# Loading and multiplying the late modulation weights in steps between the projections of a two-layer diffusion transformer

## The chip, the cores and the metric

The kernel runs as one program on one core of one Trainium2 chip. The time of a kernel is the device time of one execution in microseconds; three runs of the kernel before lie within 2729.07 to 2732.03 us, with a median of 2731.18 us. TensorE is called PE below, VectorE DVE, ScalarE ACT, GpSimd POOL, and SyncE, which issues the transfers spoken of here, SP.

## What is computed

Two layers (`DEPTH = 2`) work on 1024 tokens and 256 context tokens of 1024 features in fp32. Cut to what matters:

```python
for l in range(DEPTH):
    m_lat = jnp.split(_adaln(c, w_mod[l], b_mod[l])[:, None, :], N_MOD, axis=-1)
    m_ctx = jnp.split(_adaln(c_ctx, w_mod[l], b_mod[l]), N_MOD, axis=-1)
    h = _modulate(_rmsnorm(x, norm1_w[l]), m_lat[0], m_lat[1])
    hc = _modulate(_rmsnorm(cx, norm1_w[l]), m_ctx[0], m_ctx[1])
    mix, mix_c = _token_mixers(h, hc, w_in[l], ...)
    x = x + m_lat[2] * jnp.einsum('btm,md->btd', mix, w_out[l])
    h2 = _modulate(_rmsnorm(x, norm2_w[l]), m_lat[3], m_lat[4])
    x = x + m_lat[5] * _expert_choice_ffn(h2, w_router[l], ...)
    ...
def _adaln(cond, w, b):
    return jnp.matmul(jax.nn.silu(cond), w) + b
def _modulate(h, shift, scale):
    return h * (1 + scale) + shift
```

`w_mod[l]` is 1024 x 6144. Its six column blocks of 1024 give, for two condition vectors, the shift and scale of the first norm (part 0 in the kernel), the gate of the mixers and the shift of the second norm (part 1), and the scale of the second norm and the gate of the experts (part 2). Only part 0 is needed before the mixers; parts 1 and 2 are first used after the attention, when `w_out` has been applied. The mixers are a projection by `w_in`, a gated linear recurrence (three pairs of heads), a short convolution, and an attention over a neighbourhood of 8 x 16 (three pairs of heads).

## The kernel before

The main loop (lines 1430 to 1500) takes a layer in stages. First the normed and modulated tokens are kept transposed as a high and a low half (`hh`, `hl`), so that a product in fp32 is made of three products in a faster format. **Projections:** `wgroup` (L243) loads a group of 256 columns of `w_in` in two halves of 512 KB (tile `wst`, three buffers), ACT casts each half to `whi` (L264), DVE subtracts to `wlo` (L265). `proj_ch` (L277) or `proj_tok` (L288) then run 24 matmuls per output tile, `pj`, and ACT or DVE moves the result out through tiles of the ring `ev` (three buffers, `nev` at L566) to DRAM. There are 15 such groups: two for the recurrence's values (the first one's weights are loaded ahead), six for its three pairs, three for the convolution, and four, in `na_proj` (L585), for the attention. The recurrence (`hg_pair`: `hl`, `hds`, `ho`, then the mean of squares `hms` at L504 in the PSUM bank "E", its root and reciprocal `hrs`, and the output `hos`) runs beside the projections of what follows.

**Attention:** `na_consts` (L591) loads the norm weights `naw` and the rotation tables `cw` and `sw`; `na_prep` (L647) loads queries and keys `qk`, norms and rotates them on DVE and POOL (`nss`, `nrs...`, `qn`, `qd`) and has PE transpose them (`nt`, L697). `na_pair` (L771) makes scores (`sA`, `sB`), adds the bias on DVE (L743), takes the exponential on ACT (L750), transposes (`npt`) and multiplies by the values (`nao`). The preparation of the next pair is written behind each pair and overlaps with it. After pair 0 and the preparation of pair 1 stands `adaln(l, [1, 2], ap)`: two parts of eight steps (k = 0 to 7), each with two loads of 512 KB of `w_mod` (tile `wm`, L153, four buffers in a pool of its own that is opened after the projections' pools are closed) and four matmuls `aps` of 128 x 512 (L157; eight records in the trace) in the four column groups of PE, then the sum with the bias (`ms`, L166, with `bt`, L160 to 162), its store, and transposes and copies to `mt` and `AB` (L168 to 178). The part 0 of layer 0 is made at the program's start, that of layer 1 among the experts of layer 0.

The order on each engine is set by a scheduler at build time: it may move an instruction ahead of others on its engine, but every engine then runs its own list strictly in that order, and waits on semaphores for the others. A tile of a ring can be filled only when the use of the tile before it in the same buffer is over. In order of time the stages of the profiled execution are: projections and recurrence of layer 0 from 22 to 616 us, pair 0 to 722, pair 1 to 794; in layer 1 from 1500 to 2010, 2142 and 2218 us.

## Time and profile before

| | before |
|---|---|
| median of three runs | 2731.18 us |
| the profiled execution's own time | 2732.13 us |
| span of its profile | 2730.4 us |
| PE busy | 2504.4 us (92%) |
| DVE busy | 1884.3 us (69%) |
| ACT busy | 1131.4 us (41%) |
| POOL busy | 669.3 us (25%) |
| moved by DMA | 507.12 MB, 186 GB/s in the mean |

Busy time is the time in which an engine ran at least one instruction, as a share of the span; matmuls overlap, and the end of one is modelled, so that a busy PE need not be at its peak. An engine's share is a mean over stages that have different limits: what a change is worth is read from the rows of the stretches that it touches.

### The profile page before, as it was taken

The page shows a single profiled execution, that of the slowest core. Times are in us where ns is not written, and L with a number is a line of the kernel's source. Part 1 is how long each engine was busy: PE and PEld are TensorE (multiplying, and loading weights), DVE is VectorE, ACT ScalarE, POOL GpSimd, SP SyncE. Part 2 cuts the span into 40 slices and gives each one's busy share as a digit, 9 for nine tenths or more (in the row PEclk, how much of TensorE's full clock was granted, in tenths as well). Part 3 has the DMA queues.
Part 4 walks back from the last instruction along what each step waited for, and adds up shares of the span by engine and source line. Part 5 has one row for each costly group of instructions (what it writes and reads, how often), then busy time and mean ns, then how long its engine had stood idle before and what let it go on. Part 6 is the DMA issues. An engine that isn't in the chain of part 4 may idle for free.

```text
span 2730.4 us, 55190 instructions
## 1 busy us (share of the span) xinstructions
PE 2504.4 (92%) x21959; PEld 1906.9 (70%) x21959; DVE 1884.3 (69%) x4046; ACT 1131.4 (41%) x1878; POOL 669.3 (25%) x621
## 2 busy tenths in 40 slices
PE   7999999998999979999996999999958899589997
PEld 4998887894677855555554988778844677367664
DVE  4258887857666586777754368787858874787874
ACT  4224433324554534444434334333314554345452
POOL 1000000035444633333311000000045532222241
PEclk9999999998999979999998999999979999789999
DMA  7332324247354948888887332423176355889994
GB/s 281 102 108 71 114 68 123 66 138 243 113 160 135 349 151 278 281 280 279 283 280 212 94 105 74 124 84 89 49 200 225 94 163 183 300 281 370 377 376 127
DMA packets 347936, 507.12 MB, mean 186 GB/s; under 512 B 53380, under 2 KB 203072, under 8 KB 346592
## 3 DMA queue, kind: packets, MB, share of 16 engines
q1 hardware_dynamic: 336416, 465.85, 50.4%
q0 software_dynamic: 11264, 37.75, 5.9%
q8 instruction: 173, 2.83, 0.4%
q14 instruction: 83, 0.68, 0.1%
HBM read 410.10 MB, written 94.90 MB: 185 GB/s over the span
## 4 chain that ended last, share of the span: by engine, by line
PE 67%; DVE 18%; DMA 5%; issue 4%; ACT 3%; POOL 2%; SPq 1%; POOLq 0%; DVEq 0%; ACTq 0%
PE pg L1280 13%; PE pj L277 12%; PE pd L1335 8%; PE pj L288 8%; PE po L828 6%; PE nao L786 3%; PE pgc L1265 2%; PE npt L762 2%; PE sA L733 1%; DVE Kt L375 1%; PE aps L157 1%; DVE Kt L376 1%; DVE Qt L378 1%; PE hl L365 1%; PE xt L1231 1%
## 5 line engine op out<-in xcount | busy, mean ns | idle before, releaser
L1182 DVE TENSOR_TENSOR ewl<-est,ewh 128x2048 fp32r<-128x2048 f32 x126 | 298.1, 2371 | 109.7 <-ACT ewh L1178 108.6
L1178 ACT CAST ewh<-est 128x2048 fp32r<-128x2048 f32 x128 | 243.4, 1905 | 170.9 <-PE pg L1280 130.5
L277 PE MATMUL pj<-hl,whi 128*128 128x320 f32 (+2 forms) x912 | 310.2, 340 | 0.0
L277 PE MATMUL pj<-hh,whi 128*128 128x320 f32 (+2 forms) x912 | 309.9, 340 | 0.0
L277 PE MATMUL pj<-hh,wlo 128*128 128x320 f32 (+2 forms) x912 | 308.7, 339 | 0.0
L288 PE MATMUL pj<-whi,hh 128*128 128x256 f32 x960 | 277.8, 290 | 4.5 <-ACT nev L566 4.1
L288 PE MATMUL pj<-whi,hl 128*128 128x256 f32 x960 | 276.8, 291 | 0.8 <-DVE hl L239 0.8
L288 PE MATMUL pj<-wlo,hh 128*128 128x256 f32 x960 | 275.5, 288 | 0.0
L1335 PE MATMUL pd<-est,hidT 128*128 128x512 f32 x512 | 232.2, 596 | 2.1 <-ACT hidT L1302 2.1
L288 PEld LDWEIGHTS pj<-whi,hh 128*128 128x128 f32 x960 | 186.0, 194 | 8.8 <-ACT nev L566 5.2
L288 PEld LDWEIGHTS pj<-wlo,hh 128*128 128x128 f32 x960 | 185.9, 194 | 2.2 <-issue 1.3
L288 PEld LDWEIGHTS pj<-whi,hl 128*128 128x128 f32 x960 | 184.6, 194 | 3.5 <-issue 1.3
L277 PEld LDWEIGHTS pj<-hh,whi 128*128 128x128 f32 x912 | 172.2, 189 | 13.7 <-issue 0.9
L277 PEld LDWEIGHTS pj<-hl,whi 128*128 128x128 f32 x912 | 172.2, 189 | 13.5 <-issue 1.9
L277 PEld LDWEIGHTS pj<-hh,wlo 128*128 128x128 f32 x912 | 172.1, 189 | 13.0 <-issue 1.1
L1335 PEld LDWEIGHTS pd<-est,hidT 128*128 128x128 f32 x512 | 95.2, 189 | 110.7 <-issue 103.3
L265 DVE TENSOR_TENSOR wlo<-wst,whi 128x1024 fp32r<-128x1024 f32 (+1 forms) x72 | 75.2, 1058 | 131.7 <-ACT whi L264 130.6
L1280 PE MATMUL pg<-ewh,xh 128*128 128x512 f32 x512 | 156.8, 424 | 3.1 <-ACT xh L1235 3.0
L752 POOL TENSOR_SCALAR S<-S,sm 128x768 f32<-128x768 f32 (+2 forms) x108 | 108.6, 1007 | 188.3 <-DVE sm L751 166.8
L1280 PE MATMUL pg<-ewl,xh 128*128 128x512 f32 x512 | 147.7, 404 | 0.0
L1280 PE MATMUL pg<-ewh,xo 128*128 128x512 f32 x512 | 142.3, 398 | 2.1 <-DVE xo L1236 2.1
L750 ACT ACTIVATE S<-S,mn 128x768 f32<-128x768 f32 (+2 forms) x108 | 98.6, 913 | 85.2 <-DVE mn L745 79.6
(369 smaller groups left out, 5560.9 us busy)
## 6 DMA issues: line engine op xcount, KB each, us to landing
est<-in_w_exp_gate_dram SPq DMA_DIRECT2D x64, 1024.0 KB
est<-in_w_exp_up_dram SPq DMA_DIRECT2D x64, 1024.0 KB
est<-in_w_exp_down_dram SPq DMA_DIRECT2D x64, 1024.0 KB
wm<-in_w_mod_dram SPq DMA_DIRECT2D x80, 512.0 KB
wst<-in_w_in_dram SPq DMA_DIRECT2D x88, 256.0 KB
pna<-nev SPq DMA_DIRECT2D x180, 64.0 KB
wos<-in_w_out_dram SPq DMA_DIRECT2D x42, 256.0 KB
mst<-mix SPq DMA_DIRECT2D x32, 320.0 KB
```

Of the source, the lines that this page charges most:

```text
L265: nc.vector.tensor_tensor(b, c, a, ALU.subtract)
L277: nc.tensor.matmul(ps[:, :cn], sel(a(k)), b[:, k, c0:c0 + cn], start=n == 0, stop=n == 3 * KD - 1)
L288: nc.tensor.matmul(ps[:, :2 * P], b[:, k, t * P:(t + 1) * P], a(k).rearrange("p a n -> p (a n)"), start=n == 0, stop=n == 3 * KD - 1)
L750: nc.scalar.activation(S[:, :w], S[:, :w], AF.Exp, scale=-1.0, bias=mn[:, 1:2], accum_out=sm[:, 0:1])
L752: nc.gpsimd.tensor_scalar(S[:, :w], S[:, :w], sm[:, 1:2], 1.0, ALU.mult, ALU.mult)
L762: nc.tensor.transpose(pt[:kn, i], S[:, c:c + kn], self.idf)
L786: nc.tensor.matmul(po[64 * X:64 * X + 64, gi], V[:kn, tt, 64 * X:64 * X + 64], PT[X][:kn, i], start=i == 0, stop=i == len(ch) - 1, tile_po ...
L828: nc.tensor.matmul(ps, a, b, start=n == 0, stop=n == len(ops) - 1)
L1178: nc.scalar.copy(hi, src)
L1182: nc.vector.tensor_tensor(lo[:, :m], src[:, :m], hi[:, :m], ALU.subtract)
L1280: nc.tensor.matmul(acc[gu], a[:, 4 * hf + k], b[:, 512 * k:512 * k + 512], start=n == 0, stop=n == 3 * KD - 1)
L1335: self.downed = nc.tensor.matmul(po[nn], hT[:, 2 * hf + k], st[:, c:c + 512], start=hf == 0 and k == 0, stop=hf == 1 and k == 1)
```

## The change

Parts 1 and 2 of the modulation are taken out of the attention. A generator, `adaln_steps`, makes one of its sixteen steps (two loads, four matmuls) each time that it is called. `wgroup` calls it once after the loads of its group, and the convolution twice more. The two tiles of a step now come from the ring `wst` of the projections' weights, `aps` accumulates in bank "E", and the bias and sum tiles `bt` and `ms` come from the ring `ev`. The mean of squares `hms` moves from bank "E" to bank "D", where `ho` is. The pool `ad1` with its four buffers is gone. The bytes loaded, the matmuls and the vector work are the same. Part 0 is computed as before.

```diff
+    def adaln_steps(self, l, wp):
+        nc, I = self.nc, self.I
+        for r in (1, 2):
+            ps = self.bank("E", [P, 512], F32, "aps")
             for k in range(KD):
                 w = []
...
+                for h in (0, 1024):
+                    t = wp.tile([P, 1024], F32, name="wm", tag="wst", bufs=3)
+                    nc.sync.dma_start(t, I["w_mod"][l, k * P:(k + 1) * P, r * 2048 + h:r * 2048 + h + 1024])
+                    w += [t[:, a:a + 512] for a in (0, 512)]
+                self.adaln_mm(ps, k, w)
+                if k == KD - 1:
+                    bt, ms = [wp.tile([P, 512], F32, name=n, tag="ev", bufs=3) for n in ("bt", "ms")]
+                    self.adaln_end(l, r, ps, bt, ms, "E")
+                yield
...
@@ def wgroup
+        next(self.side, None)
         return (lambda k: his[k // 4][:, k % 4]), (lambda k: los[k // 4][:, k % 4])
...
@@ def hg_pair
-            pm = self.bank("E", [P, 512], F32, "hms")
+            pm = self.bank("D", [P, 512], F32, "hms")
...
@@ def conv_proj
             w = self.wgroup(l, wp, c, c + P)
+            if c != CB0:
+                next(self.side)
...
@@ def mixers_in
         self.hg_consts(self.hp)
+        self.side = self.adaln_steps(l, wp)
...
@@ main loop
-        adp = K.pool(f"ad1_{l}", side="right")
-        ap = adp.__enter__()
...
-                    if p == 0:
-                        K.adaln(l, [1, 2], ap)
-            adp.__exit__(None, None, None)
```

The line numbers of the changed file differ: `aps` is L145, its loads L198, `pj` L304 and L315, `hms` L532, `nt` L727, the transfers of `naw`, `cw`, `sw`, `qk` L626 to L691.

On PE, among the recurrence's projections of layer 0, the changed kernel has at one place (a row counts an instruction, of which the trace shows two records for fp32 `aps`):

```order
L304 MATMUL pj<-hh,whi 128x320
L304 MATMUL pj<-hl,whi 128x320
L304 MATMUL pj<-hh,wlo 128x320
L145 MATMUL aps<-wm,sT 32x512 x4
L304 MATMUL pj<-hh,whi 128x320
L304 MATMUL pj<-hl,whi 128x320
```

A whole step stands there in one piece between two groups of columns; before, nothing stood between such `pj`. Of the 32 steps of both layers, most stand like this; the first two of each layer are split in halves, and a few others 1 + 3.

On PE at the end of layer 1's projections, before, behind the last `hms` come 46 `pj`, and behind the last of them:

```order
L288 MATMUL pj<-whi,hl 128x256
L157 MATMUL aps<-wm,sT 32x512 x8
L697 MATMUL nt<-idf,qd 128x128 x4
L157 MATMUL aps<-wm,sT 32x512 x8
L697 MATMUL nt<-idf,qd 128x128 x8
L157 MATMUL aps<-wm,sT 32x512 x2
```

In the changed kernel 105 `pj` come behind the last `hms`, and then:

```order
L315 MATMUL pj<-whi,hl 128x256
L727 MATMUL nt<-idf,qd 128x128 x20
L765 MATMUL sB<-KH,QT 128x256
L765 MATMUL sB<-KL,QT 128x256
L727 MATMUL nt<-idf,qd 128x128 x16
```

The modulation is gone from the first transposes of the attention, and the end of the recurrence has moved ahead, against the projections.

On SP in the same place, before, behind the last store of a projection:

```order
L510 DMA mix_15766<-hos 128x512
L869 DMA wr<-in_w_router_dram 128x8x16
L637 DMA E<-rpbx 64x14x64 x4
L596 DMA naw<-in_na_q_norm_dram 128x64
L597 DMA naw<-in_na_k_norm_dram 128x64
L609 DMA cw<-in_rope_dram 128x4x64
```

and in the changed kernel:

```order
L537 DMA mix_15762<-hos 128x512
L597 DMA pna_15763<-nev 128x128 x2
L626 DMA naw<-in_na_q_norm_dram 128x64
L627 DMA naw<-in_na_k_norm_dram 128x64
L639 DMA cw<-in_rope_dram 128x4x64
L640 DMA sw<-in_rope_dram 128x4x64
L597 DMA pna_15763<-nev 128x128 x2
```

The loads for the attention (`naw`, `cw`, `sw`) now stand ahead of the last stores of the projections, and the bias loads `E` no longer stand ahead of them.

## Rows read from the trace of the kernel before

**Rows 1.** Chain of waits, 600 to 735 us, shares of 135 us by line.

```profile
by line: PE aps L157 17.4%; PE nao L786 12.5%; PE npt L762 8.9%; POOL qd L688 6.9%; PE nt L697 6.5%; PE sA L733 6.0%; issue 4.6%; DMA qk<-pna 3.7%; PE sB L735 3.5%; DVE qn L672 3.4%; DVE QT L702 3.1%; DVE nss L664 2.6%; DVE S L743 2.5%; DMA
```

**Rows 2.** Windows: stretch, length, busy PE, PEld, DVE, ACT, POOL, clock, DMA share, GB/s.

```profile
22.00:616.00 594.00, 564.33 (x7167) 516.06 (x7166) 403.85 (x924) 229.71 (x470) 45.91 (x63) 0.99 0.37 111
1500.00:2010.00 510.00, 491.99 (x6497) 438.95 (x6495) 364.55 (x844) 186.47 (x391) 24.45 (x37) 1.00 0.30 91
...
649.00:714.00 65.00, 63.93 (x446) 35.22 (x443) 47.56 (x122) 27.90 (x54) 29.96 (x30) 1.00 0.65 211
2072.00:2111.00 39.00, 38.32 (x255) 19.99 (x255) 33.70 (x76) 16.55 (x30) 21.60 (x19) 1.00 0.65 209
```

**Rows 3.** The same windows for L157 alone: stretch, length, busy PE, PEld.

```profile
616.00:722.00 106.00, 32.09 (x128) 4.39 (x128) 0.90 0.69 214
2010.00:2142.00 132.00, 33.19 (x128) 4.59 (x128) 0.86 0.68 199
...
649.00:714.00 65.00, 24.69 (x104) 3.43 (x100) 1.00 0.65 211
2072.00:2111.00 39.00, 15.80 (x64) 2.17 (x64) 1.00 0.65 209
```

**Rows 4.** PE's waits, 100 to 616 and 1500 to 2010 us: in total, times, longest.

```profile
PE hl L341 <- DVE Qt L378: 7.5, 11, 1.3
...
PE hl L341 <- DVE Qt L378: 12.6, 17, 1.7
```

**Rows 5.** Timeline of PE: start, us, line, operation, records; half and whole steps.

```profile
659.68 1.05 PE L157 MATMUL aps<-wm,sT 128*32 128x512 f32 x4
660.66 1.09 PE L786 MATMUL nao<-PT,nav 128*64 128x128 f32 x16
...
1453.33 1.06 PE L157 MATMUL aps<-est,sT 128*32 128x512 f32 x8
...
2058.91 1.07 PE L157 MATMUL aps<-wm,sT 128*32 128x512 f32 x8
```

**Rows 6.** Timeline of ACT: exponentials of scores in pairs 0 and 1, both layers.

```profile
649.00 0.94 ACT L750 ACTIVATE S<-S,mn 128x768 f32<-128x768 f32 x1
...
706.07 0.99 ACT L750 ACTIVATE S<-S,mn 128x832 f32<-128x832 f32 x1
...
730.64 0.98 ACT L750 ACTIVATE S<-S,mn 128x768 f32<-128x768 f32 x1
...
767.81 0.99 ACT L750 ACTIVATE S<-S,mn 128x832 f32<-128x832 f32 x1
...
2072.30 0.94 ACT L750 ACTIVATE S<-S,mn 128x768 f32<-128x768 f32 x1 [4.28 <-DVE mn L745]
...
2111.59 0.99 ACT L750 ACTIVATE S<-S,mn 128x832 f32<-128x832 f32 x1
...
2149.44 0.94 ACT L750 ACTIVATE S<-S,mn 128x768 f32<-128x768 f32 x1
...
2172.60 0.99 ACT L750 ACTIVATE S<-S,mn 128x832 f32<-128x832 f32 x1 [0.88 <-DVE mn L745]
```

**Rows 7.** Timeline of PE, SP and DVE at the end of layer 1's projections.

```profile
2002.73 1.02 PE L505 MATMUL hms<-hsq,hones 128*128 128x512 f32 x2
...
2008.98 0.28 PE L288 MATMUL pj<-whi,hl 128*128 128x256 f32 x1
...
2045.23 1.11 PE L697 MATMUL nt<-idf,qd 128*128 128x128 f32 x4 [2.84 <-DVE qd L688]
...
2021.73 0.89 SPq L596 DMA_DIRECT2D naw<-in_na_q_norm_dram  x1
...
2032.08 1.06 DVE L672 TENSOR_TENSOR qn<-qk,cw 128x512 f32<-128x512 f32 x1 [4.98 <-DMA qk<-pna]
```

**Rows 8.** Timeline: one half group of weights from issue to cast.

```profile
1465.42 0.96 SPq L252 DMA_DIRECT2D wst<-in_w_in_dram  x2
...
1469.72 1.04 ACT L264 CAST whi<-wst 128x1024 fp32r<-128x1024 f32 x1 [11.28 <-DMA wst<-in_w_in_dram]
```

More of the change, by code (lines that the diff above doesn't have):

```diff
@@ L134, in bounds, with adaln_open, adaln_mm @@
         nc.vector.tensor_scalar(self.lb1, self.lb, -1.0, 1.0, ALU.mult, ALU.add)
-    def adaln(self, l, parts, ap, tag="M", bufs=4, late=None, big=None):
+    def adaln_open(self, l):
+        self.mds[l] = self.dram(f"mod{l}", [2, 6 * D])
+        self.mts[l] = self.cp.tile([P, 2, 48], F32, name=f"mt{l}")
+        self.ABs[l] = self.cp.tile([P, 2, 2, KD], F32, name=f"ab{l}")
+    def adaln_mm(self, ps, k, w):
+        for j in range(4):
+            self.nc.tensor.matmul(ps[32 * j:32 * j + 32], self.sT[:, k, :], w[j], start=k == 0, stop=k == KD - 1,
+                                  tile_position=(0, 32 * j))
@@ L139, in adaln, with adaln_end @@
+    def adaln_end(self, l, r, ps, bt, ms, tag, late=None):
         nc, I = self.nc, self.I
[L140 to L143 removed]
         md, mt, AB = self.mds[l], self.mts[l], self.ABs[l]
[L145 to L147 removed]
+        nc.gpsimd.memset(bt, 0.0)
+        for j in range(4):
+            nc.sync.dma_start(bt[32 * j:32 * j + 2],
+                              I["b_mod"][l:l + 1, (4 * r + j) * 512:(4 * r + j + 1) * 512].to_broadcast([2, 512]))
+        if late:
+            late()
+        nc.vector.tensor_tensor(ms, ps, bt, ALU.add)
+        for j in range(4):
+            nc.sync.dma_start(md[:, (r * 4 + j) * 512:(r * 4 + j + 1) * 512], ms[32 * j:32 * j + 2])
+        tp = self.bank(tag, [P, 4, P], F32, "atp")
+        for c in range(4):
+            nc.tensor.transpose(tp[:, c], ms[:, c * P:(c + 1) * P], self.idf)
+        for i in range(2):
+            nc.vector.tensor_copy(mt[:, i, r * 16:(r + 1) * 16].rearrange("p (j c) -> p j c", j=4),
+                                  tp.rearrange("p c (j q) -> p j c q", j=4)[:, :, :, i])
+            if r != 1:
+                s, nm = (0, "n1") if r == 0 else (1, "n2")
+                nc.vector.scalar_tensor_tensor(AB[:, i, s], mt[:, i, (3 * s + 1) * 8:(3 * s + 2) * 8], 1.0,
+                                               self.vec(nm, 8 * l, 8), op0=ALU.add, op1=ALU.mult)
@@ new lines, in adaln @@
+    def adaln(self, l, ap, tag="M", bufs=4, late=None, big=None):
+        nc, I = self.nc, self.I
+        self.adaln_open(l)
+        ps = self.bank(tag, [P, 512], F32, "aps")
+        self.modlds = []
+        for k in range(KD):
+            w = []
+            n = 2048 if big else 1024
+            for h in range(0, 2048, n):
+                t = big() if big else ap.tile([P, n], F32, name="wm", bufs=bufs)
+                self.modlds.append(nc.sync.dma_start(t, I["w_mod"][l, k * P:(k + 1) * P, h:h + n]))
+                w += [t[:, a:a + 512] for a in range(0, n, 512)]
+            self.adaln_mm(ps, k, w)
+        bt, ms = [ap.tile([P, 512], F32, name=n, tag=t if big else n, bufs=1) for n, t in (("bt", "sc0"), ("ms", "sc1"))]
+        self.adaln_end(l, 0, ps, bt, ms, tag, late)
```

43 lines of the change are left out of this document (5 added, 38 removed).

## The prediction, made before the changed kernel was run

> **What bounds the kernel now.** I read the chain of waits first, then the windows, then the waits of PE, then single records in the timeline. The chain around layer 0's pair 0 has `aps` at its head: 17.4% of 135 us, 23.5 us, are modulation matmuls that PE had to finish before something else could go on [rows 1]. The windows say why: between 649 and 714 us PE is busy for 63.93 of 65 us, and 24.69 of these are `aps`; DVE is busy for only 47.56 [rows 2, 3]. In layer 1 the like stretch, 2072 to 2111 us, has PE at 38.32 of 39 us, 15.80 of it `aps`, and DVE at 33.70. So pair 0 is bound by PE while the modulation runs beside it.
>
> The place to which the work goes is bound by PE too: 564.33 of 594 us in layer 0's projections, 491.99 of 510 in layer 1's [rows 2]. That leaves 29.7 and 18.0 us in which PE does nothing, in crumbs: its largest single cause is the wait for `Qt` from DVE, 11 waits of together 7.5 us and 17 of together 12.6 us, none over 1.7 us [rows 4]. The transfers, on the contrary, have room there (shares of 0.37 and 0.30, against 0.65 in pair 0). So this is no move from a full engine to an idle one: it takes matmuls from one PE-bound stretch to another, and what it is worth depends on how many matmul-microseconds the work takes in each place, and on what bounds the attention next.
>
> **Cost in the projections.** A half step (four records, two column groups) takes PE from 659.68 to 660.66, 0.98 us, before the next operation starts; a whole step of eight records takes 1.07 us, the same as a half [rows 5]. In the attention most stand as halves, which is why 128 records take 32.09 and 33.19 us in the two layers [rows 3]. In the changed order most steps stand whole. Sixteen whole ones take 16 x 1.07 = 17.1 us per layer; two are split in halves (+1 us each) and about three 1 + 3 (+0.5 each), which makes some 20 us per layer. The other end is that all stand as halves: 16 x 2.1 = 33.6 us; the end below is that PE's waits, 29.7 and 18.0 us, take the steps in, and the cost is near nothing. I take 15% as hidden in those waits, because the steps stand at borders of groups and not where PE waits for `Qt`: 17 us per layer. To that come waits for weights that arrive late. A half group needs 4.30 us from issue to cast [rows 8], and a step takes two of the three staging buffers. In the order at least 100 matmuls lie between most buffers' release and their use, 14 us at the 0.14 us apiece in which 46 `pj` run from 2002.73 to 2008.98 [rows 7], so that these transfers are covered; at about three places per layer the distance is short, and I allow 1 us in layer 0 and none in layer 1 beyond what the hidden share covers. Together **18 us in layer 0 and 17 in layer 1**.
>
> The vector and store work of `ms`, `mt` and `AB` (some ten short operations a layer) moves onto a DVE that is busy for 68% and 71% of the projections; I price it at nothing, and if that cover fails it shows as more waits of `hl` for `Qt`. `hms` in the bank of `ho` makes the next `ho` wait for the root of the mean; it stands tens of `pj` apart in PE's order, so nothing as well. SP issues the same 32 loads a layer, now among stores of projections, where no load of the critical chain stands behind them except the next group's weights, priced above.
>
> **Gain in layer 0's attention.** Without `aps`, PE would need 63.93 - 24.69 = 39.2 us for 649 to 714, less than DVE's 47.56, so the gain can't be all 24.7. The pace is read from the exponentials: with the modulation 11 intervals between 649.00 and 706.07, 5.2 us each; in pair 1, which has the same work and the next pair's preparation but no modulation, 9 between 730.64 and 767.81, 4.1 us each [rows 6]. At pair 1's pace 65 us become 51: 14 us. Of the 7.4 us of `aps` before 649 I count 1, since the preparation on DVE and POOL sets the time there. **15 us**; the ends are 0 (the preparation of pair 1 takes the place of the matmuls) and 23.5, the chain's share.
>
> **Gain in layer 1.** The pace goes from 4.9 us (8 intervals from 2072.30 to 2111.59) towards pair 1's 3.3 (7 from 2149.44 to 2172.60) [rows 6]; I take 3.6, nearer to the second, which is the same work, and get 39 x (1 - 3.6/4.9) = **10 us**. Of the 17.4 us of `aps` outside that stretch [rows 3] some delay the transposes `nt` and what follows: ends 0 and 8, I take **4 us**.
>
> The rest is at the start. PE stands still for the attention from 2008.98 to its first transpose at 2045.23, 36.3 us [rows 7]. The `aps` at its head don't cause that. The last `hms` is at 2002.73; `naw` is issued 19.0 us later, at 2021.73, because its buffer is free only when the recurrence's last output has been stored; from there to `nt` it is 23.5 us. In the new order 105 instead of 46 `pj` follow the last `hms`, so the tail of the recurrence runs 59 x 0.14 = 8 us earlier against the end of the projections. Further, the loads of `naw`, `cw` and `sw` go out between the last stores, and those of `qk` right behind them, with no bias loads ahead and no modulation weights beside them. `qn` came 10.4 us after `naw`; if the square roots no longer follow it, `nt` comes some 4 us after it: that is 19.0 + 10.4 + 4 = 33.4 us after `hms`, of which 105 x 0.14 = 14.3 are projections, so 19 us after PE's last projection instead of 36. That would be 17; the shift of the tail alone gives 8. I take **14 us**, nearer to the upper end, less a few for `qk`, whose loads still wait for the last stores.
>
> **Sum.** Layer 0: 15 - 18 = -3. Layer 1: 10 + 4 + 14 - 17 = +11. The profiled execution took 2732.1 us and would take 2724.1; that execution is 0.95 us above the median of the runs, so the forecast against the median is **2723 us**, 8 us faster. Under 0.2%, about 5.5 us, a measurement of this kernel can't tell a change from none.
>
> **A rule that speaks against it.** The nearest rows show no price for a change between operations of different column width: eight `aps` between transposes and scores at 2058.91 take 1.07 us, eight among nothing but `aps` at 1453.33 take 1.06 [rows 5]. By the Trainium skill, "TensorEngine Tiling (Array Packing)", section Key Properties, a change of tiling mode drains the engine, and every step here goes from whole-array matmuls to 32-column ones and back. By that rule the overlap of neighbouring matmuls would be lost at each change; these rows don't show it, but they don't have `pj` at both sides. It is the rival D below, priced from rows.
>
> **Rivals.**
> - **L, larger gain.** The steps fall into PE's waits: if a step before a wait for `Qt` only takes up that wait, 23 of the 35 us of cost vanish, and the time is 2700. For it: 47.7 us of idle PE in the two stages. Against it: the waits are under 1.7 us each and DVE's lists follow PE's.
> - **D, drain.** A `pj` lasts 0.28 us and starts every 0.14; if the overlap is lost at both sides of 32 steps, that is 64 x 0.14 = 9 us, and the time is 2732: no change.
> - **N, the start of layer 1 stays late.** The shift of 8 us comes, but the rotation tables and the square roots still stand in line on DVE and POOL, and pair 0's pace falls less: 6 us of the 14, 5 of layer 0's 15 and 2 of layer 1's 10 are lost: 2736.
> - **S, slower: weights late at the borders of groups.** Its place is the ring of three staging buffers: the second half of a group's weights can be loaded only when the step before it has been multiplied, which stands in PE's own list behind the running group. It decides if the distance in PE's list is shorter than load and cast, 4.3 + 1.0 us [rows 8], so under some 40 `pj`. I counted six such places in the two layers; at 4.3 us each, with nothing gained back, that is 26 us, less the one already in the sum: 2748. For it speaks that a group needs four tiles of the ring with its step; against it, that most distances exceed 100 `pj`.
>
> **Chances and range.** The forecast's own case, 2712 to 2734, has 0.48; L 0.14, D 0.10, N 0.14, S 0.14. Faster by over 0.2% is 0.6 of the first case and L: 0.29 + 0.14 = 0.43, and 0.01 of D makes 0.44. Within 0.2% are a third of the first (0.16), 0.08 of D and 0.04 of N: 0.28. Slower are 0.03, 0.01, 0.10 and 0.14: 0.28. The range reaches to L's centre less a little and to just short of S: 2700 to 2744; half of L and most of S lie outside. The two unknowns that make it wide are the hidden share of the steps (0 to 35 us of cost) and the bound of the attention without them.
>
> **What would show it.** Right: the projections of layer 0 longer by 16 to 20 us, with `aps` of 16 to 20 us in them and PE's waits there little changed; pair 0 of layer 0 shorter by 12 to 17 us with DVE near its limit; exponentials at 4.1 and 3.6 us in pair 0; the gap from PE's last projection to the first `nt` of layer 1 near 20 us. Wrong: stages of the projections that grow by less than 10 us (L) or more than 25 (S, then with waits of `pj` on `whi` or of `whi` on `wst`); `pj` next to `aps` that start late (D); a gap at layer 1's start that stays over 28 us (N).

## The result and the profile after

The changed kernel takes **2776.06 us** in the median of four runs (2769.85 to 2777.78), the kernel before 2730.15 us on the same chip (2729.07 to 2732.03): a ratio of 1.0163, with a 95% interval of 1.0146 to 1.0181. It is slower by 1.6%, some 46 us, where 8 us less were forecast; the time lies outside the range of 2700 to 2744.

The profiled execution of the changed kernel has a span of 2776.1 us. Cut at the first and last record of the matmul lines on PE, the two spans compare as follows (us). `pg` are the experts' products for tokens, on all 128 columns of PE; `pgc`, further down, are those for context tokens, in groups of 32 columns:

| stretch | before | after | difference | forecast |
|---|---|---|---|---|
| start to the last `pj` of layer 0 | 616.0 | 644.8 | +28.8 | +18 |
| from there to the first `pg` of layer 0's experts | 389.7 | 383.8 | -5.9 | -15 |
| first to last `pg` of layer 0's experts | 422.6 | 433.0 | **+10.4** | 0 |
| to the first `pj` of layer 1 | 50.7 | 50.6 | -0.1 | 0 |
| first to last `pj` of layer 1 | 530.0 | 552.0 | +22.0 | +17 |
| to the first `nt` of layer 1 | 36.2 | 20.9 | -15.3 | -14 |
| from there to the end | 685.2 | 691.0 | **+5.8** | -14 |
| sum | 2730.4 | 2776.1 | +45.7 | -8 |

One number held, the start of layer 1's attention. Every other term was too favourable, and one stretch that the prediction does not mention, in code that the change does not touch, lost 10 us.

The windows of the changed kernel (columns as in [rows 2]): both stages of projections, the head of pair 0 in either layer in two pieces each, and 100 us of layer 0's experts.

```profile
22.00:645.00 623.00, 590.55 (x7301) 522.28 (x7299) 397.48 (x922) 233.01 (x472) 45.65 (x64) 0.98 0.43 133
1512.00:2064.00 552.00, 532.10 (x6780) 462.19 (x6781) 387.79 (x901) 203.90 (x422) 32.64 (x50) 0.99 0.40 125
...
648.00:680.00 32.00, 16.85 (x58) 11.44 (x58) 30.06 (x56) 13.58 (x29) 18.42 (x18) 0.50 0.42 108
680.00:716.00 36.00, 29.90 (x208) 21.78 (x207) 30.07 (x70) 18.64 (x37) 23.29 (x20) 0.88 0.11 34
2085.00:2112.00 27.00, 11.54 (x42) 8.28 (x42) 24.28 (x33) 10.49 (x18) 14.04 (x12) 0.50 0.21 55
2112.00:2145.00 33.00, 26.89 (x181) 19.20 (x181) 30.37 (x73) 16.39 (x31) 20.57 (x18) 0.85 0.11 32
1123.00:1223.00 100.00, 100.00 (x517) 50.57 (x516) 70.76 (x93) 40.59 (x42) 27.10 (x20) 1.00 0.84 276
```

The same for the line of `aps` alone:

```profile
22.00:645.00 623.00, 28.30 (x146) 4.19 (x144) 0.98 0.43 133
1512.00:2064.00 552.00, 20.99 (x128) 3.26 (x128) 0.99 0.40 125
```

The `aps` cost what was worked out: 28.30 us less the 5.7 us of part 0 that layer 0 had before is 22.6, and 20.99 in layer 1, against 20. But nothing of the steps fell into PE's waits: PE's idle time in layer 0's projections is now 32.5 us where it was 29.7 [rows 2]. In layer 1 it is 19.9 us where it was 18.9 over the like stretch, from the first to the last `pj` (the window of [rows 2] begins 21 us later). Before:

```profile
1479.00:2009.00 530.00, 511.08 (x6646) 457.73 (x6646) 383.24 (x890) 203.51 (x421) 29.03 (x43) 0.99 0.32 96
```

In the heads of the attention, 648 to 680 and 2085 to 2112 us, DVE is busy for 30.06 of 32 and 24.28 of 27 us, and the clock granted to PE is 0.50, the lower of its two levels.

### The profile page after: what moved, and what is told of

Read it like the earlier page. It is cut to its first block, busy times and chain, and to the rows that moved or that the text cites. A ratio compares the mean times of both kernels' runs of the same rounds, so it can differ in the third digit from the quotient of the medians.

```text
span 2776.1 us, 55178 instructions
## 1 busy us (share of the span) xinstructions
PE 2522.9 (91%) x21959; PEld 1919.2 (69%) x21959; DVE 1880.9 (68%) x4046; ACT 1135.7 (41%) x1880; POOL 652.0 (23%) x621
## 4 chain that ended last, share of the span: by engine, by line
PE 54%; DVE 14%; DMA 3%; issue 2%; ACT 1%; POOL 1%; SPq 1%; POOLq 0%; DVEq 0%; ACTq 0%
PE pg L1310 13%; PE pd L1365 8%; PE po L858 6%; PE pj L304 5%; PE pj L315 4%; PE nao L816 2%; PE pgc L1295 2%; PE npt L792 2%; PE sA L763 1%; DMA wst<-in_w_in_dram 1%; PE xt L1261 1%; PE pdc L1371 1%; DVE mg L1050 1%; DVE qd L718 1%; DVE Kt L402 1%
## 5 line engine op out<-in xcount | busy, mean ns | idle before, releaser
L304 PE MATMUL pj<-hh,wlo 128*128 128x320 f32 (+2 forms) x912 | 311.3, 341 | 0.0
L304 PE MATMUL pj<-hh,whi 128*128 128x320 f32 (+2 forms) x912 | 311.0, 341 | 0.0
L304 PE MATMUL pj<-hl,whi 128*128 128x320 f32 (+2 forms) x912 | 308.9, 339 | 0.0
L315 PE MATMUL pj<-whi,hh 128*128 128x256 f32 x960 | 278.8, 291 | 1.9 <-ACT nev L595 1.6
L315 PE MATMUL pj<-wlo,hh 128*128 128x256 f32 x960 | 277.1, 289 | 0.0
L315 PE MATMUL pj<-whi,hl 128*128 128x256 f32 x960 | 276.1, 291 | 0.1
L315 PEld LDWEIGHTS pj<-whi,hh 128*128 128x128 f32 x960 | 186.8, 195 | 12.4 <-ACT nev L595 6.4
L304 PEld LDWEIGHTS pj<-hh,whi 128*128 128x128 f32 x912 | 173.0, 190 | 27.0 <-issue 8.1
L315 PEld LDWEIGHTS pj<-whi,hl 128*128 128x128 f32 x960 | 185.5, 195 | 4.2 <-issue 1.8
L315 PEld LDWEIGHTS pj<-wlo,hh 128*128 128x128 f32 x960 | 186.9, 195 | 2.0 <-issue 1.0
L304 PEld LDWEIGHTS pj<-hh,wlo 128*128 128x128 f32 x912 | 173.0, 190 | 14.6 <-issue 2.3
L304 PEld LDWEIGHTS pj<-hl,whi 128*128 128x128 f32 x912 | 173.0, 190 | 13.1 <-issue 1.8
```

Of the source, the lines that this page charges most:

```text
L304: nc.tensor.matmul(ps[:, :cn], sel(a(k)), b[:, k, c0:c0 + cn], start=n == 0, stop=n == 3 * KD - 1)
L315: nc.tensor.matmul(ps[:, :2 * P], b[:, k, t * P:(t + 1) * P], a(k).rearrange("p a n -> p (a n)"), start=n == 0, stop=n == 3 * KD - 1)
```

## The experiments

Fifteen kernels ran, in four groups, each group beside fresh runs of the kernel before. Ratios are to those. Stage lengths are cut as in the table above; between the profiled executions of two kernels with the same order in a stage they differ by 0 to 2 us in most stages. The kernel before has one trace, of 2730.4 us; beside the later groups its median was 2733.5 to 2736.9 us, so stages that are compared with that trace add up to 3 to 7 us more than the medians differ.

### Where does it come from: one layer, one bank, none at all

**Layer 1 alone.** In layer 0 the modulation stays beside pair 0.

```diff
-        self.side = self.adaln_steps(l, wp)
+        self.side = self.adaln_steps(l, wp) if l in (1,) else iter(())
```

`hms` moves to bank "D" in layer 1 alone, too.

> Steps in the projections in layer 1 alone; layer 0 as before, its experts in the order of before. If the loss is the sum of local terms read from the changed kernel's trace (layer 1's projections +22 us, its start -15 us, the rest of its attention 0, its experts 0 to +5), the time is 7 to 12 us above before: 2737 to 2742. If the +10 us of layer 0's experts were no effect of the order of instructions there but something that any use of the steps brings, 2747 to 2752.

Measured: ratio 1.0026 (1.0016 to 1.0035), 2743.76 us beside 2736.85, +7 us. Layer 0's experts took 422.6 us, exactly as before; layer 1's projections +24, its start -14.6, the rest +1. The local terms add up, and the loss in layer 0's experts does not come with steps in layer 1.

**Layer 0 alone** (the same with `l in (0,)`, for the bank as well).

> Steps in layer 0 alone; layer 1 as before. Local terms: projections +29 us, attention -5 us, experts of layer 0 in the changed order +10 us: 34 us above before, 2764. If the experts' +10 us were chance of one execution, 24 us above, 2754.

Measured: ratio 1.0155 (1.0136 to 1.0174), 2780.48 us, +44 us and 10 more than expected. Projections of layer 0 +32, attention and output -8, experts +10.4; layer 1, in which nothing is edited, takes 13 us more from its first transpose to its first `pg`. The experts' 10 us are no chance of one execution: the stage takes the same 433.0 us.

**The bank alone.** The kernel before, one letter changed.

```diff
-            pm = self.bank("E", [P, 512], F32, "hms")
+            pm = self.bank("D", [P, 512], F32, "hms")
```

> The kernel before with the mean of squares in the bank of ho, and nothing else. Its experts of layer 0 come out in the changed kernel's order of instructions, although nothing in them is edited. If that order costs, their stage takes about 433 instead of 423 us and the time is about 2740; if the order is worth nothing and the bank neither, 2730; a wait of ho for the root of the mean would show as PE waiting for hrs in the projections, 2 to 5 us.

Measured: ratio 1.0067 (1.0046 to 1.0088), 2757.08 us, **20 us by the medians for one bank**. The experts of layer 0 took 432.7 us, as in the changed kernel. The first transpose of layer 0 came 12 us after the last `pj`, where before it came at once. Layer 0's projections took 583.7 us from the first to the last `pj`, where before they took 579.3. The direct wait for the bank is small; of PE's waits in layer 0's projections it is one line (total, times, longest):

```profile
PE ho L493 <- ACT hrs L507: 2.5, 1, 2.5
```

So most of what the bank costs is what the scheduler makes of it far away. The order of layer 0's experts on PE differs between this kernel and the one before, and is the same as in the changed kernel.

**Left out.** Parts 1 and 2 are not computed; the values of part 0 stand in for them.

> Parts 1 and 2 of the modulation are left out (no loads, no matmuls; the values of part 0 are used in their place). Clock theory: without aps PE is granted the lower clock for 40 to 55 us at the head of each attention, as in the changed kernel, so from the first transpose to the first output matmul layer 0 takes about 146 us (before 154.5) and layer 1 about 134 (before 134): hardly any gain, and PE's 65 us of aps were nearly free where they stood. The forecast's theory: about 139 and 120. The gap at layer 1's start stays near 36 us if the order of the recurrence's tail decides it, and falls to 21 if the modulation's loads decided it.

Measured: ratio 1.0034 (1.0019 to 1.0048), 2745.47 us. With 33.6 MB of loads and 65 us of matmuls **less**, the kernel is slower than before. Layer 0's attention is 12.7 us shorter, from its first transpose to its first output matmul. In layer 1 that stretch is 135.4 us against 134.0, and the gap ahead of it 37.3 against 36.2. Layer 0's experts took 443.7 us, 21 more than before, in yet another order. The head of layer 1's attention without any modulation, in two windows:

```profile
2063.00:2089.00 26.00, 11.66 (x45) 8.50 (x45) 21.95 (x34) 9.29 (x15) 11.96 (x11) 0.57 0.18 51
2089.00:2132.00 43.00, 38.52 (x266) 28.95 (x266) 38.17 (x101) 23.54 (x44) 25.29 (x22) 0.81 0.10 32
```

DVE is busy for 38.17 of 43 us. So layer 1's 33 us of modulation matmuls had cost nothing where they stood, beside DVE's preparation and scores. And the gap at layer 1's start did not come from the modulation's loads, as the forecast had it: in this kernel, too, the router's and the bias loads go out ahead of `naw` on SP, and the gap stays.

### The attention: clock or DVE

**Idle matmuls in the old place**, in the changed kernel.

```diff
+    def filler(self):
+        for r in range(2):
+            ps = self.bank("M", [P, 512], F32, "fil")
+            for k in range(KD):
+                self.adaln_mm(ps, k, [self.CW[:, :512]] * 4)
...
                     ops = K.na_prep(l, p + 1, nt, (nk, nk1)[(p + 1) % 2], "E")
+                    if p == 0:
+                        K.filler()
```

They are 64 matmuls a layer of the form of `aps`, on a table that is in place.

> The changed kernel with 128 idle matmuls of the form of aps (no loads, result unused) where the modulation stood before, beside pair 0 of each layer: 65 us more of PE's work in all. Clock theory: PE gets the higher clock back sooner (low for about 20 to 28 us at each head instead of 41 and 55), so the attention of each layer grows by at most 10 us in layer 0 and 0 to 5 in layer 1. If the clock there is worth nothing, PE's 32 us per layer come on top as they did before: +10 to +15 us per layer.

Measured: ratio 1.0173 (1.0152 to 1.0193), 2782.87 us. The test did only half of what it was for: with no loads to wait for, the scheduler put layer 1's idle matmuls into the gap ahead of the attention, not beside pair 0. In layer 0 most stand at the head of the attention; the clock was low there for 17 us instead of 41, and the attention was 4 us longer than in the changed kernel, within the 10 us that the clock theory allowed. That does not decide it, since the matmuls did not stand beside pair 0.

**Idle matmuls at the head.**

```diff
+            if hp_ == 0 and l == DEPTH - 1:
+                fp = self.bank("M", [P, 512], F32, "fil")
+                for _ in range(8):
+                    nc.tensor.matmul(fp[:, :n * P], self.idf, qk[:, 0].rearrange("p t c -> p (t c)"), start=True, stop=True)
...
+            if hp_ < 2:
+                fp = self.bank("M", [P, 512], F32, "fil")
+                for _ in range(4):
+                    nc.tensor.matmul(fp[:, :n * P], self.idf, qn[:, 0].rearrange("p t c -> p (t c)"), start=True, stop=True)
```

> The changed kernel with idle matmuls only at the head: 24 on the loaded queries and keys while PE waits for layer 1's first transposes, and 12 among the transposes of the first two pairs of each layer. Clock theory: the low stretch of layer 1 (55 us) shrinks to 30 or less and the attention of layer 1 loses 5 to 10 us, so the time is 2766 to 2772 where the changed kernel takes 2776. If DVE sets the time there (it is busy for 30 of 33 us behind the first exponential), the clock comes back and the time stays within 3 us or grows by the filler's own 5.

Measured: ratio 1.0222 (1.0196 to 1.0248), 2793.54 us. The clock was there (1.00 in the first window) and layer 1's attention was 17 us longer than in the changed kernel, where one theory expected 5 to 10 us less and the other at most 5 more. The windows, and below them the filler's part of PE:

```profile
2089.00:2116.00 27.00, 19.31 (x64) 10.03 (x65) 15.95 (x20) 6.30 (x11) 11.75 (x8) 1.00 0.18 50
2116.00:2149.00 33.00, 27.11 (x110) 16.54 (x108) 27.22 (x51) 12.38 (x21) 14.01 (x15) 0.79 0.14 40
```

```profile
2089.00:2116.00 27.00, 16.40 (x40) 7.29 (x40) 1.00 0.18 50
2116.00:2149.00 33.00, 13.48 (x24) 6.34 (x24) 0.79 0.14 40
```

The filler took 29.9 us of PE in these two windows and the attention grew by 17. A higher clock at the head did not by itself make the stretch shorter; how much of the filler's 29.9 us it paid back can't be read from this, since the filler stands in PE's list ahead of the transposes.

### The projections: matmuls or loads

**Matmuls alone** (with parts 1 and 2 left out, the steps' matmuls on a constant).

> Parts 1 and 2 left out as in the run before, but the sixteen steps' matmuls stand in the projections, multiplying a constant; no modulation loads anywhere. If a step's price is PE's alone (1.18 us for a whole step with the two changes of column width), the projections of each layer are 19 to 24 us longer than with all left out. If the loads in the ring make the loss, 10 or less.

Measured: 2748.83 us in one run. Inconclusive for the price of a step: with nothing to wait for, all 128 matmuls were scheduled at the program's start and between the two layers, none among the projections. But like the next two runs, and unlike the one with all left out, this kernel has `hms` in bank "D", so it serves as a second base for them: first to last `pj` 583.8 and 530.8 us, with all left out 581.6 and 532.7.

**Loads alone.**

```diff
+    def adaln_steps(self, l, wp):
+        for r in (1, 2):
+            for k in range(KD):
+                for h in (0, 1024):
+                    t = wp.tile([P, 1024], F32, name="wm", tag="wst", bufs=3)
+                    nc.sync.dma_start(t, I["w_mod"][l, k * P:(k + 1) * P, r * 2048 + h:r * 2048 + h + 1024])
+                yield
...
```

> Parts 1 and 2 left out, but the steps' 32 loads of 512 KB per layer go through the ring of the projections' weights; no matmuls of the modulation. PE theory: the projections are 0 to 4 us longer than with all left out. Ring theory (weights late at the borders of groups): 10 us or more, with PE or ACT waiting for wst.

Measured: 2769.57 us in one run. First to last `pj`: +7 us in layer 0 and +16 in layer 1 against the kernel with all left out, +5 and +18 against the one with the matmuls elsewhere. ACT waits for `wst` 3.8 us in layer 0 and not in layer 1, PE in neither. Layer 1's projections, without loads and with them:

```profile
1493.00:2026.00 533.00, 513.03 (x6642) 458.46 (x6642) 381.91 (x890) 204.71 (x424) 30.42 (x45) 0.99 0.33 96
```

```profile
1501.00:2050.00 549.00, 521.46 (x6642) 465.85 (x6642) 383.59 (x891) 206.74 (x425) 31.87 (x46) 0.97 0.42 125
```

The same 6642 matmuls take 8.4 us more of PE, at a clock of 0.97 instead of 0.99 (it was at the lower level for 32 us instead of 8), and PE stands idle 7.5 us longer. So neither theory fits. The loads are not late, and PE's waits for `Qt` are even shorter (7.0 us instead of 12.4); but there are waits that were not there, 4.6 us of `ho` for the root `hrs`, which the bank brings, and 6.7 for the recurrence's queries (`Qt<-q`) and for a tile that ACT empties (`pev`). Each of the six pieces of lower clock lies at a wait of PE of 1.1 to 3.8 us. That the loads bring these waits by the order, and not in another way, is not shown.

**Matmuls pinned.** The steps' matmuls multiply the tile `wst` of the group at hand, no loads.

```diff
+                w = self.lastst.rearrange("p k a n -> p (k a n)")
+                self.adaln_mm2(ps, k, [w[:, 512 * (j % 2):512 * (j % 2) + 512] for j in range(4)])
...
```

> Parts 1 and 2 left out, no loads of the modulation; the sixteen steps' matmuls multiply the group's own staged weights, which holds them at the borders of the groups. If PE's own time is the price (1.2 us a step and the split ones), the projections of each layer are 19 to 24 us longer than with all left out. If the loads make most of it, under 10 in layer 1.

Measured: 2756.47 us in one run; first to last `pj` 17 us longer in layer 0 and 15 in layer 1 than with all left out, 15 and 17 against the other base. That is near the 17.1 us of sixteen whole steps at 1.07, with little or nothing hidden. In layer 0, 17 and the loads' 7 make the 25 us that the changed kernel needs over the one with all left out, in which the bank is counted twice; against the other base 15 and 5 make 20 of 23. In layer 1 they make 31 where the changed kernel needs 19, so the loads' price there does not carry over from that one run.

### The experts: order and width

In all runs I took the start of each PE record to the start of the next, and what this takes more at a change from one kind of matmul to another than among records of the same operands. Four `pgc` that start together, one in each column group, count as one and take 0.42 us, and the late start of the second matmul behind a change is counted with the change. In layer 0's experts:

| kernel | changes of width | lost at one, ns | lost at a change of kind alone, ns | first to last `pg`, us |
|---|---|---|---|---|
| before, layer 1 alone | 150 | 154 | 19 | 422.6 |
| changed, layer 0 alone, bank alone | 192 | 163 | 25 | 432.7 to 433.0 |
| loads alone, filler in the old place | 200 | 161 | 29 | 435.0 and 432.8 |
| left out | 204 | 164 | 32 | 443.7 |

(In PE's order, in which a row may hold several, the counts are 163, 207, 215 and 219.) A change between matmuls on all 128 columns (`pg`, `pd`, `xt`) and on 32 (`pgc`, `pdc`, `hcp`) loses 0.16 us, one to 32 columns and back 0.3; one between two kinds of the same width loses 0.02 to 0.03. One such place in the kernel before:

```profile
1154.87 4.45 PE L1335 MATMUL pd<-est,hidT 128*128 128x512 f32 x10
1159.25 1.92 PE L1265 MATMUL pgc<-est,xct 128*32 128x512 f32 x16
1161.10 2.84 PE L1335 MATMUL pd<-est,hidT 128*128 128x512 f32 x6
1163.78 0.17 PE L1148 MATMUL slp<-pay,O 128*128 128x5 bf16 x1
```

A `pd` starts every 0.429 us among `pd`; here ten take 4.38 us up to the first `pgc` and six 2.68, 0.09 and 0.11 more than that. The four expectations that follow price a change at 0.28 us, which is too much: that figure takes the 7 ns between two `pgc` that start together as the normal spacing, and so counts the run of a last group, 0.42 us, as lost. The 443.7 us of the kernel with all left out are not the width alone: the clock was at its lower level for 19.6 us of that stage, where it was 8.2 before.

This led to an edit that changes only where `pgc` is written:

```diff
                     late.append((gu, hf, st))
-                    if len(late) > 1 * first:
+                    while hf == 1 and len(late) > 1 * first:
                         ctx_mm(*late.pop(0))
```

for pairs, and without the two lines (all four behind both weights) for quads, in the kernel before and in the changed one.

> The kernel before, with the experts' context matmuls pgc of both halves of a weight written one behind the other. In PE's order of layer 0's experts the changes between whole-array and 32-column matmuls fall from 163 to 133. Width theory (0.28 us lost at each change, as the spacing of records in the earlier runs shows): that stage takes 423 - 8 = 415 us, and the time is 8 us below before. If the stage's length in the earlier runs came from something else (transfers, the chip), it stays at 423 or gets longer, since weights are held longer.

> The same edit in the changed kernel: width changes in layer 0's experts fall from 207 to 155. Width theory: the stage takes 433 - 14 = 419 us and the time falls by 14 us against the changed kernel. If the steps' cost is elsewhere: no change.

> The kernel before, all context matmuls of an expert's gate and up written behind both: 113 width changes instead of 163. Width theory: 423 - 14 = 409 us. Against it: the staging of the weights is freed later, so loads go out later; if PE then waits for weights, the stage is longer than 423.

> The same in the changed kernel: 107 width changes instead of 207. Width theory: 433 - 28 = 405 us for the stage and about 28 us off the changed kernel's time.

| kernel | changes of width | first to last `pg`, expected | measured | first `pg` to the first `pj` of layer 1 | median | ratio to before |
|---|---|---|---|---|---|---|
| before | 150 | | 422.6 | 473.3 | | |
| changed | 192 | | 433.0 | 483.6 | | |
| before, pairs | 122 | 415 | 416.5 | 468.0 | 2740.12 | 1.0018 (1.0008 to 1.0028) |
| changed, pairs | 144 | 419 | 427.6 | 479.1 | 2763.78 | 1.0100 (1.0082 to 1.0118) |
| before, quads | 102 | 409 | 411.5 | 466.9 | 2741.11 | 1.0024 (1.0013 to 1.0036) |
| changed, quads | 96 | 405 | 410.9 | 466.4 | 2754.14 | 1.0071 (1.0052 to 1.0090) |

The stage gets shorter with the count, and that the measured lengths come near to the expected ones with quads is in part luck: 24 of the 504 `pgc` records of the stage then stand behind the last `pg`, its end mark. Up to the first `pj` of layer 1, a mark that no edit moves, quads gave 6.4 us in the kernel before and 17.2 in the changed one, 0.13 and 0.18 us per change, which agrees with the 0.16 of the spacings. The changed kernel with pairs is an outlier: 29 groups of its `pgc` are torn into three and one, and a lone `pgc` takes as long as four side by side, so that `pgc` keeps PE busy for 76.7 us in this kernel and for 69.0 in the changed one. In the windows PE is busy for 100 of 100 us in every one of these kernels, and what tells them apart is how many matmuls it started meanwhile: 536 before, 517 in the changed kernel, 543 with quads. Before, and before with quads:

```profile
1100.00:1200.00 100.00, 100.00 (x536) 53.36 (x535) 72.97 (x98) 40.41 (x41) 30.04 (x20) 1.00 0.83 271
```

```profile
1106.00:1206.00 100.00, 100.00 (x543) 55.43 (x544) 71.37 (x100) 42.09 (x43) 29.87 (x22) 1.00 0.84 278
```

But **the time did not follow the stage** in the kernel before: with pairs and quads the experts gave 5.3 and 6.4 us, and layer 1's attention, which nobody edited, took 8.5 and 9.4 us more from first to last transpose. The medians are 6 and 7 us above before.

### Two tries at a version that beats both

**Layer 1's steps with quads**, and **the kernel before with quads and a convolution that waits for the recurrence's end** in layer 1:

```diff
         for hf in range(2):
-            self.conv(l, hf, ds)
+            with self.tc.issue_after(self.lasthos.ins) if l == 1 and hf in (0, 1) else nullcontext():
+                self.conv(l, hf, ds)
...
```

> Steps in layer 1 alone, and the experts' context matmuls of gate and up written behind both (113 width changes in layer 0's experts). By the stages: 7 us above before for the steps in layer 1, 11 below for the experts, so 4 us below before if layer 1's attention keeps its length; if it takes 131 us as in the two runs of before with the new order of the experts, 4 us above.

> The kernel before with the context matmuls written behind both, and layer 1's convolution held behind the recurrence's last output on DVE, so that the tail of the recurrence is over earlier. Experts 11 us shorter; the gap at layer 1's start falls from 36 us by up to 8 if DVE's queue made the tail late, and stays if the convolution's own tiles now free the buffer late.

Measured: 2751.39 us, ratio 1.0055 (1.0038 to 1.0072), and 2751.56 us, ratio 1.0057 (1.0040 to 1.0074). From first to last `pg` the experts gave 8 and 12 us (up to the first `pj` of layer 1, 3 and 7). In the first, layer 1's start gave 15.6 and its projections and what follows took it back; in the second the gap at layer 1's start grew by 7 us, so the theory of DVE's queue fell: in SP's list two late stores of the convolution (`mix<-cy`, 2026.27 us) now stand ahead of `naw` (2031.05). None of the fifteen kernels is faster than the one before.

## Why the prediction was wrong

The time came out 53 us above the forecast. No single step of it failed alone: the terms of the sum that were mis-sized follow in the order of time, the largest being layer 1's attention (nothing instead of 14), the projections (51 us instead of 35) and the experts (10 us instead of nothing).

**Projections: the step that failed is "I take 15% as hidden in those waits".** The steps' own price, some 20 us per layer, measured 22.6 and 21. Hidden was nothing: PE's idle time there grew by 2.8 and 1.0 us. In layer 1 these two make the whole 22.0. In layer 0 some 4 us more go to the bank, by the run with the bank alone, which the prediction had put at "nothing as well", and 1.7 lie ahead of the first `pj`; the mean clock there is 0.98 instead of 0.99, which may hold part of this. Weights that come late, which were to cost 1 us in layer 0, cost 2.7 in three waits of `aps`. The wait for `Qt` [rows 4] did not shrink in layer 0, and in layer 1 went from 12.6 to 11.1. Layer 0's projections from 60 us on (total, times, longest):

```profile
PE hl L368 <- DVE Qt L405: 8.3, 10, 2.5
...
PE aps L145 <- DMA wm<-in_w_mod_dram: 2.7, 3, 1.8
```

**Rival D was the right mechanism, at nearly its price, and the sum held most of it already.** One step in layer 0's projections of the changed kernel:

```profile
143.25 0.31 PE L304 MATMUL pj<-hl,whi 128*128 128x320 f32 x1
143.40 0.31 PE L304 MATMUL pj<-hh,wlo 128*128 128x320 f32 x1
143.63 1.07 PE L145 MATMUL aps<-wm,sT 128*32 128x512 f32 x8
144.63 0.41 PE L304 MATMUL pj<-hh,whi 128*128 128x320 f32 x1
144.88 0.30 PE L304 MATMUL pj<-hl,whi 128*128 128x320 f32 x1
145.02 0.31 PE L304 MATMUL pj<-hh,wlo 128*128 128x320 f32 x1
```

`pj` follows `pj` after 0.15 us; `aps` follows after 0.23, and the second `pj` behind it after 0.25. A whole step moves the list by 1.18 us (1.08 to 1.28 in the ten whole steps that stand between `pj`). Where `aps` follow `aps` with nothing between, in part 0 of layer 1 in the kernel before, a step takes less, 4.42 us for forty records or 0.88 for eight:

```profile
1448.65 4.49 PE L157 MATMUL aps<-est,sT 128*32 128x512 f32 x40
1453.07 0.33 PE L1317 MATMUL hct<-idf,hidc 64*128 64x64 f32 x2
1453.33 1.06 PE L157 MATMUL aps<-est,sT 128*32 128x512 f32 x8
1455.01 1.06 PE L157 MATMUL aps<-est,sT 128*32 128x512 f32 x8 [0.61 <-DMA est<-in_w_mod_dram]
```

So the two changes of a step cost 0.30 us, and D's price for them was 0.28. But the sum had taken 1.07 us for a step, and that holds 0.19 of them: over the sum a step costs 0.11, 3.5 us in all, and not 9. The row that was to speak against D was misread: the eight `aps` at 1453.33 are not "among nothing but `aps`", they stand between a transpose and a wait. The Trainium skill, "TensorEngine Tiling (Array Packing)", section Key Properties, says that a change of tiling mode drains the engine. The trace agrees, with 0.3 us for a change to 32 columns and back, in these projections and in the experts; the page gives no price.

**The experts: a term that was missing.** Every edit was priced where it stands, the bank of `hms` at "nothing as well". Alone it cost 20 us, of which 2.5 are the wait that was looked for. The order of all engines is one schedule of the whole program, and it came out different in a stage that begins 380 us behind the edit. There the new order has 42 more changes of width: 42 x 0.16 = 7 us. Added up record by record, changes lose 23.7 us before and 32.2 in the changed kernel, 8.5 of the 10.4 us, and PE's waits in the stage are 1.3 us longer. That could be read blind: the order of the experts in the two kernels shows 163 and 207 changes of width. I read the orders only at the places that are edited.

**Layer 0's attention: 5.9 us instead of 15.** The mechanism was right and the size was not. From the first transpose to the first output matmul it is 8.7 us shorter, and the first transpose comes 3.2 us after the last `pj`, where before it came at once. With the modulation left out that stretch is 12.7 us shorter, and in the other kernels with the same steps in layer 0 (layer 0 alone, pairs, quads) 10.8 to 12.8. So the matmuls had cost some 13 us there, near the 15, and the changed kernel's own order gave part of that back. The step "at pair 1's pace" was too favourable for a reason that can be read: in pair 1 the queries of pair 1 are ready and only pair 2's are prepared; pair 0 starts behind its own preparation, and without `aps` that stretch is DVE's: 30.06 of 32, then 30.07 of 36 us [rows 2 had 47.56 of 65]. At the same time PE got the lower clock for 41 us, where it had been 20 before; which of the two sets the time there is not shown. The count was off too: from 649.00 to 706.07 there are 10 intervals, not 11.

**Layer 1's attention: nothing instead of 14.** The step that failed is the same, "nearer to the second, which is the same work". It compared the slow part of pair 0 with the fast part of pair 1. From 2072.30 to 2111.59 there are 7 intervals, not 8; and over whole pairs, before, the 16 exponentials of pair 0 span 63.2 us beside the modulation and those of pair 1 67.6 us without it. Last of pair 0, first and last of pair 1, before:

```profile
2135.48 0.93 ACT L750 ACTIVATE S<-S,mn 128x768 f32<-128x768 f32 x1 [1.50 <-DVE mn L745]
2142.11 0.94 ACT L750 ACTIVATE S<-S,mn 128x768 f32<-128x768 f32 x1 [2.36 <-DVE mn L745]
...
2209.74 0.94 ACT L750 ACTIVATE S<-S,mn 128x768 f32<-128x768 f32 x1 [2.83 <-DVE mn L745]
```

So no gain could be read from pair 1's pace. The exponentials of the changed kernel, first and last of pair 0 and first of pair 1:

```profile
2112.84 0.94 ACT L780 ACTIVATE S<-S,mn 128x768 f32<-128x768 f32 x1 [3.56 <-DVE mn L775]
...
2172.21 0.94 ACT L780 ACTIVATE S<-S,mn 128x768 f32<-128x768 f32 x1
...
2182.43 0.93 ACT L780 ACTIVATE S<-S,mn 128x768 f32<-128x768 f32 x1
```

Pair 0's fifteen intervals take 59.4 us, 4.0 each, so the pace did improve by 4 us in all; then pair 1 begins 10.2 us later, where it was 6.6. The chain from 2085 to 2173 us shows what stands there now:

```profile
by line: issue 8.8%; POOL nro L709 8.5%; POOL qd L718 8.4%; DVE qn L702 7.2%; DVE qd L718 6.9%; DMA nav<-pna 6.3%; PE npt L792 6.2%; DVE nss L694 5.5%; DVE S L773 5.0%; PE nao L816 4.7%; DVE qn L711 4.4%; DVE S L775 4.1%; DVE KL L735 3.8%; 
```

The preparation (`qd`, `qn`, `nro`, `nss`) on DVE and POOL has taken the place of `aps`; this was the first of the ends that I named for layer 0, "the preparation of pair 1 takes the place of the matmuls", and I gave it the weight of an end and not of a case. With the modulation left out, the same stretch gained nothing either, which shows that layer 1's 33 us of `aps` were nearly free where they stood. The 5.8 us that are lost from the first `nt` to the end lie for the most part behind the attention: from its first output matmul to the first `pg` of layer 1 it is 226.8 us instead of 222.0, in code that no edit touches, and why is not shown.

**Layer 1's start: the right number, 15.3 us against 14, in part by luck.** PE and SP at the end of layer 1's projections in the changed kernel:

```profile
2050.87 1.02 PE L532 MATMUL hms<-hsq,hones 128*128 128x512 f32 x2
...
2064.20 0.28 PE L315 MATMUL pj<-whi,hl 128*128 128x256 f32 x1
2085.11 1.09 PE L727 MATMUL nt<-idf,qd 128*128 128x128 f32 x4 [20.63 <-issue]
```

```profile
2057.51 0.32 SPq L537 DMA_DIRECT2D mix<-hos  x1
2059.20 0.80 SPq L597 DMA_DIRECT2D pna<-nev  x2
2060.16 0.33 SPq L626 DMA_DIRECT2D naw<-in_na_q_norm_dram  x1
...
2067.30 3.18 SPq L691 DMA_DIRECT2D qk<-pna  x6
...
2071.55 7.88 SPq L667 DMA_DIRECT2D E<-rpbx  x4
```

The shift in the order came as forecast, 7.1 us where 8 were expected: the last `hms` now stands 13.3 us ahead of the last `pj`, before 6.3. The rest was to come from `naw` to `nt`, 14.4 us instead of 23.5; that gave nothing, it takes 25. In its place from the last `hms` to `naw` it is 9.3 us instead of 19.0 [rows 7], which the forecast had left at 19.0. Two misses of some 10 us cancelled each other. Of the 9.7 us, 5.1 are the last store of `hos`, which goes out sooner, and 4.6 lie between it and `naw`, where before the four loads of `E` stood on SP:

```profile
2014.44 0.68 SPq L510 DMA_DIRECT2D mix<-hos  x1
...
2015.72 5.91 SPq L637 DMA_DIRECT2D E<-rpbx  x4
```

That the order and not the modulation's loads made the gap is shown by the kernel with all left out, where the gap is 37 us, and by the one with pinned matmuls and no loads, where it is 16; with the matmuls elsewhere, or the loads alone, it is 34 and 33.

The pieces: projections +16 us over the forecast, layer 0's attention +9, the experts +10, layer 1's attention and the rest +20, layer 1's start -1: together 54 us, between the 2724.1 us of the sum and the 2777.8 of the profiled execution. **The slower rival, S,** did occur where I put it, in the ring, and cost little: in the changed kernel the casts on ACT wait for their weights in both layers, by these two waits of ACT (layer 0's projections, then layer 1's behind the first group; total, times, longest), where before it was 2.0 us in layer 0 and none behind layer 1's first group:

```profile
ACT whi L290 <- DMA wst<-in_w_in_dram: 34.3, 14, 5.2
...
ACT whi L290 <- DMA wst<-in_w_in_dram: 43.4, 11, 7.2
```

But ACT is busy for 37% of that time, and `pj` itself waits for `wst` 0.3 us in all: the distance in PE's list covers it, as the argument against S had it.

What stays open: how much of the attention's head the lower clock costs by itself, how the scheduler comes from one bank to another order of the experts, and why layer 1's attention takes 123 us in one order and 132 in another, with the same instructions.

## What to carry to other kernels

Where a scheduler orders the whole program, an edit is never local: compare the two orders in every stage, not only where the edit stands, and count what is dear there (here changes of matmul width). Each of the fifteen versions here was slower than the kernel before, those with less work too; that its order is a lucky one, and that a change must first pay for losing it, fits this but is not shown. Work beside a stretch that another engine fills can be nearly free (33 us in layer 1 here); before moving it, ask what its engine would do there instead, by leaving it out altogether in one run. A pace that is read from part of a stage has to be held against the whole stage. And where PE's idle time is made of waits of a microsecond behind another engine's chain, work put between them added its full price here.

## What the runs showed of the hardware that was not expected

A change between matmuls on 128 and on 32 columns lost 0.15 to 0.16 us, and 0.3 us to 32 columns and back, among fp32 matmuls of 512 columns in the experts as well as around the steps between projections of 320 columns; a change of kind at the same width lost 0.02 to 0.03. A lone `pgc` of 32 columns took as long as four in the four column groups, some 0.43 us. With less work on PE its granted clock was lower at the head of both attentions (0.50 for 41 and 55 us instead of 20 and 27), and idle matmuls that brought it back did not make the stretch shorter. In layer 1's projections the same 6642 matmuls took 8.4 us longer with small waits between them and a clock of 0.97 instead of 0.99 in the mean.
